# Dilated attention and S5 in one kernel: key loads as one tile for two heads, a gate unit in halves, S5's end behind each tile's weights

## The chip, the cores and the metric

The kernel runs on one core of one Trainium2 chip. The metric is the device time of one execution in microseconds (us); of the kernel before there are three runs, 2085.07, 2089.13 and 2091.08, median 2089.13 us.

The engines are named as in the profile: PE (TensorE, matrix products), DVE (VectorE), ACT (ScalarE), POOL (GpSimd) and SP (SyncE, which here only issues DMA transfers).

## The reference

Two transformer blocks stand one behind the other, both with width 1024 and 1024 positions. The first has dilated attention beside a Hyena branch, the second an S5 branch beside latent attention (MLA). What the change touches, cut down:

```python
# first block: 8 heads of 64, three dilations (window, step): (128, 1), (512, 4), (2048, 16)
for g, (window, d) in enumerate(DILATED_GROUPS):
    o_g, lse_g = dilated_window_attention(q[:, :, g], k[:, :, g], v[:, :, g], slopes, d, window // (2 * d))
wts = softmax(stack(lses))                      # weighs the three dilations against each other
y_attn = einsum(wts, stack(outs)) * silu(g_attn)
merged = sigmoid(r_attn) * (y_attn @ w_proj_attn) + sigmoid(r_hy) * (y_hy @ w_proj_hyena)
# second block
y = gelu(scan(u) + d_skip * u)                  # S5
ys = y * sigmoid(y @ w_glu + b_glu) * silu(gs)
ym = softmax(q @ k.T, causal) @ v * silu(gm)    # MLA, 4 heads, keys and values from a latent of 128
x = layer_norm(u + ple, ln_g, ln_b)
```

All is float32. The kernel forms each dense product as three products of halves (high by high, low by high, high by low); line 192 is the matmul of all of them.

## The kernel before, in words

The kernel is written in a tile language whose scheduler sorts the instructions of each engine by dependences and priorities; an engine then runs its own list in that order, and a DMA that SP can't issue yet holds all DMAs behind it. `tc.issue_after(ins)` ties what is traced under it behind an instruction on the same engine.

Dilated attention (`attention`, from about 750 to 1200 us) runs over four pairs of heads (hp 0 to 3) and in each over three dilations g. Queries, keys and values of g = 0 and 1 were projected earlier and lie in DRAM (`k.qkv`); those of g = 2 are projected in place, by products on PE that stand between the score tiles. The pool `qp` has two buffers of each tile, so the loads of (hp, 1) take the buffers of (hp-1, 2), and can start when that dilation's last scores are done. SP then issues for each head the queries (L1098, tile `qa`) and the keys' high and low halves (L1096, `kh` and `kl`), each as loads of 64 partitions by 1024 numbers, 256 KB: 4 of queries and 8 of keys.

In one dilation eight tiles of 128 queries are taken in pairs (`tp`) and for both heads: scores against `kh` and `kl` (L1170, L1171), bias and row minimum on DVE (L1172), exponential on ACT (L1175), transposes (L1182), the product with the values (L1186). Row minima and sums go to DRAM as `stat_d`: L1204 and L1208 for g = 0 and 1, L1212 for g = 2, the latter in pieces of 16 bytes. In the next head pair's first dilation the steps of `combined` read them back (L1023, tile `sn`) and weigh the dilations. After the first dilation of each head pair (`FILL`) one gate unit is traced (`r_unit`, 48 products, its tanh in two DMAs to `rs`, L984).

In the second block, `mla` (from about 1683 to 1860 us) walks through a list of steps: prepare a head (rotary queries `cs` and `qr`, L1933; `qn`, `kn`, L1911; values, L1972) or attend one block of 256 queries (row maxima L2000, exponential L2007, weights L2011, transposes by products L2024, output L2036). Behind each attended block some steps of S5's end (`s5_finish`, `others`) are traced: `fy` and `fu` (L1686, L1688, L1691) build the gelu, then four products with `w_glu` and their gates (L1699, L1703).

Of the kernel before, what the change touches and what calls it, by code (L numbers as in the profile page):

```python
# [9 lines left out]
F32 = mybir.dt.float32  # L10
F32R = mybir.dt.float32r
AF = mybir.ActivationFunctionType
ALU = mybir.AluOpType
# [3 lines left out]
P = 128  # L17
S = 1024
D = 1024
KD = D // P  # L20
# [15 lines left out]
def f(ap):  # L36
    return ap.bitcast(F32)
# [939 lines left out]
def r_unit(k, n, pool):  # L977

    u = UN["r_attn"] + n

    def evac(h, ps):
        t = pool.tile([P, 512], F32, name="tr", tag="tr")
        k.nc.scalar.activation(t, ps, AF.Tanh, scale=0.5, bias=k.hb[:, u : u + 1])
        k.nc.sync.dma_start(k.rs[n, :, h * 512 : (h + 1) * 512], t)  # L984

    unit(k, u, evac)


def attention(k):

    nc, tc, A = k.nc, k.tc, k.A
    k.yaT = [k.dram.tile([4, P, 512], F32, name="yaT%d" % b) for b in range(2)]
    with ExitStack() as es:
# [24 lines left out]
        def combined(hp, stat_d, w_d, og):  # L1018
# [47 lines left out]
                nc.sync.dma_start(k.yaT[b][hp], gt[:, b * 512 : (b + 1) * 512])  # L1066
            yield

        gts, pending = {}, iter(())
        for hp in range(4):  # L1070
            stat_d = k.dram.tile([3, S, 2, 2], F32, name="stat_d%d" % hp)
# [2 lines left out]
            for g in range(3):  # L1074
# [3 lines left out]

                r64 = [slice(0, 64), slice(64, 128)]
                qa, kh, kl = ([qp.tile([P, S], F32R, name=n + str(h)) for h in range(2)] for n in ("qa", "kh", "kl"))
                vT = qp.tile([P, S], F32, name="vT", bufs=1)

                def project(which):
                    u = (which * 3 + g) * 4 + hp
                    if u in k.qkv:
                        src = k.qkv[u]
                        if which == 2:
                            nc.sync.dma_start(vT, src[0])  # L1090
                            return
                        for h in range(2):
                            for part in range(2):
                                if which:
                                    for e in range(2):
                                        nc.sync.dma_start(f((kh, kl)[part][h][r64[e]]), src[part][r64[h]])  # L1096
                                else:
                                    nc.sync.dma_start(f(qa[h][r64[h ^ part]]), src[part][r64[h]])  # L1098
                        return
                    bias = k.b_in[:, u : u + 1]  # L1100

                    def evac(h, ps):
                        sl = slice(h * half, (h + 1) * half)
                        view = lambda t: t.rearrange("p (r l) -> p r l", r=d)[:, :, sl]
                        if which == 2:
                            evac_qkv(k, u, [view(vT)], ps, d)
                            return
                        ps = ps.rearrange("p (l r) -> p r l", r=d)
                        for x, r in enumerate(r64):
                            hi = view((qa, kh)[which][x])[r]  # L1110
                            lo = view(kl[x])[r] if which else view(qa[x])[r64[1 - x]]
                            nc.scalar.activation(hi, ps[r], AF.Identity, bias=bias[r])
                            nc.vector.scalar_tensor_tensor(lo, ps[r], bias[r], f(hi), op0=ALU.add, op1=ALU.subtract)

                    unit(k, u, evac)
                    if which == 1:
                        for t in (kh, kl):
                            for x in range(2):
                                nc.gpsimd.tensor_copy(t[x][r64[1 - x]], t[x][r64[x]])
# [34 lines left out]
                stat = st_.tile([P, 8, 2, 2], F32, name="stat", tag="stat")  # L1154
                o = op.tile([P, S], F32, name="og%d" % g, tag="og%d" % g, bufs=1 if g else 2)
                og.append(o)
                for tp in range(0, 8, 2):

                    po = ps_o.tile([P, 2, 2, P], F32, name="po", tag="po")
                    for h in range(2):  # L1160
                        ps = ps_s.tile([P, 2, 256], F32, name="s%d" % h, tag="s%d" % h)
                        sb = sp.tile([P, 2, 256], F32, name="sb", tag="sb")
                        for m in range(2):
                            t = tp + m
                            a, n, off, z, cs = tiles[t]
                            qt, ks = slice(t * P, (t + 1) * P), slice(a, a + n)
                            for e, rest in ((0, z), (z + n, len(cs) * P - z - n)):
                                if rest:
                                    nc.gpsimd.memset(sb[:, m, e : e + rest], 0.0)  # L1169
                            nc.tensor.matmul(ps[:, m, :n], qa[h][:, qt], kh[h][:, ks], start=True, stop=False)  # L1170
                            nc.tensor.matmul(ps[:, m, :n], qa[h][:, qt], kl[h][:, ks], start=False, stop=True)  # L1171
                            dve = nc.vector.tensor_tensor_reduce(sb[:, m, z : z + n], ps[:, m, :n], tabs[h][:, off : off + n],  # L1172
                                                           -0.125, 3.0e38, op0=ALU.add, op1=ALU.min,
                                                           accum_out=stat[:, t, h, 0:1])
                            act = nc.scalar.activation(sb[:, m, z : z + n], sb[:, m, z : z + n], AF.Exp, scale=-1.0,  # L1175
                                                 bias=stat[:, t, h, 0:1], accum_out=stat[:, t, h, 1:2])
                        nk = len(cs)
                        pst = ps_t.tile([P, 4, P], F32, name="pt", tag="pt")
                        pT = pt_.tile([P, 4, P], F32, name="pT", tag="pT")
                        for m in range(2):  # L1180
                            for x in range(nk):
                                nc.tensor.transpose(pst[:, m * nk + x, :], sb[:, m, x * P : (x + 1) * P], k.idn)  # L1182
                        copy(pT[:, : 2 * nk], pst[:, : 2 * nk])
                        for m in range(2):
                            for x, c in enumerate(tiles[tp + m][4]):
                                nc.tensor.matmul(po[:, h, m, :], vn[:, c, :], pT[:, m * nk + x, :],  # L1186
                                                 start=(x == 0), stop=(x == nk - 1))
                    for h in range(2):
                        hs = slice(h * 64, h * 64 + 64)
                        v, to = po[hs, h].rearrange("p m q -> p (m q)"), o[hs, tp * P : (tp + 2) * P]  # L1190
                        if g:
                            rr = d // 4
                            v = v.rearrange("p (r l) -> p r l", r=rr)
                            to = o[hs].rearrange("p (l r) -> p r l", r=d)[:, tp // 2 * rr : (tp // 2 + 1) * rr]
                        if h:
                            nc.scalar.copy(to, v)
                        else:
                            nc.vector.tensor_copy(to, v)  # L1198
                    if g == 0 and tp in (2, 4, 6):
                        with tc.issue_after(dve.ins), tc.issue_after(act.ins):  # L1200
                            next(pending, None)
# [7 lines left out]
                else:  # L1209
                    v = dst.rearrange("(l t r) c -> r l t c", r=2, t=8)  # L1210
                    for r in range(2):
                        nc.sync.dma_start(v[r], sv[r * 64 : r * 64 + 64])  # L1212

                if (hp, g) in FILL and late:
                    r_unit(k, late.pop(0), trp)
            pending = combined(hp, stat_d, w_d, og)
            if hp == 3:
                next(pending)
# [145 lines left out]
def product_half(k, w, r, h, evac):  # L1364

    wh, wl = w
    ps = k.pj.tile([P, 512], F32, name="pj", tag="pj")
    mm3(k.nc, ps, [(wh[:, q, :], wl[:, q, :], *r(q, h)) for q in range(wh.shape[1])])
    evac(h, ps)
# [498 lines left out]
def mla(k, others):  # L1868
# [3 lines left out]
    with ExitStack() as es:  # L1872
# [103 lines left out]
        def attend(h, b, shared=True):  # L1976
# [7 lines left out]
            for i in (2 * b, 2 * b + 1):  # L1984
# [23 lines left out]
                if two:  # L2008
                    nc.vector.tensor_add(mx[:, 2:3], mx[:, 2:3], mx[:, 3:4])
                nc.vector.reciprocal(mx[:, 4:5], mx[:, 2:3])  # L2010
                nc.vector.tensor_scalar(pb[:, :nk], pb[:, :nk], mx[:, 4:5], None, op0=ALU.mult)  # L2011
                pbs.append(pb)
            po = ps_o.tile([P, 256], F32, name="po", tag="po")
            for c in range(0, nkt, 2):
# [22 lines left out]
                                         stop=(last and m == 1 and x == 2))  # L2037
            nc.vector.tensor_mul(gm, gm, po)
            nc.sync.dma_start(k.mixm[b // 2][h, :, (b % 2) * 256 : (b % 2 + 1) * 256], gm)

        preparing = [prepare(h) for h in range(4)]
        for step in STEPS.split():
            h = int(step[1])
            if step[0] == "P":
                for _ in range(int(step[2])):
                    next(preparing[h], None)
            else:
                attend(h, int(step[2]))
                for _ in range(int(step[3])):
                    next(others, None)  # L2050

        for b in LASTB:
            attend(2, b, shared=False)
# [172 lines left out]
```

## Time and profile before

| | us |
|---|---|
| median of three runs | 2089.13 (2085.07 to 2091.08) |
| the profiled execution | 2090.47 |
| its span, first to last instruction | 2088.7 |
| PE busy in the span | 1972.1 (94%) |
| DVE, ACT, POOL busy | 1365.3 (65%), 833.1 (40%), 402.9 (19%) |
| mean granted TensorE clock | 0.98 of full speed |

A page of a profile gives busy times and groups of instructions; the waits view gives for each engine what it stood still for; the timeline lists instructions in order of time, with the idle time before each in brackets and the instruction or transfer that ended it. A queue row such as SPq is the issue of a DMA and not its flight.

### The profile page before, as it was taken

How to read it: one execution, taken by the hardware profiler on the slowest of the kernel's cores; microseconds unless marked ns; L12 is line 12 of the kernel's file. 1: busy time of each engine (PE TensorE's matmuls, PEld its weight loads, DVE VectorE, ACT ScalarE, POOL GpSimd, SP SyncE). 2: the span in 40 equal slices, each digit the busy share in tenths (PEclk: the TensorE clock that was granted, in tenths of full speed). 3: DMA queues.
4: the chain of work that ended last, by engine and by line, in shares of the span. 5: the costliest groups of instructions: out<-in, count | busy, mean ns of one | idle time of the engine just before them, and what ended most of it. 6: DMA issues, size and time to landing. Idle time of an engine off the chain costs nothing. (4 is left out here: it accounts for less than half of the span.)

```text
span 2088.7 us, 29820 instructions
## 1 busy us (share of the span) xinstructions
PE 1972.1 (94%) x10413; PEld 1653.3 (79%) x10413; DVE 1365.3 (65%) x2915; ACT 833.1 (40%) x1677; POOL 402.9 (19%) x434
## 2 busy tenths in 40 slices
PE   5999989999999999999899989998999989999997
PEld 3788777888888878878787877777777768788887
DVE  8797756788796224444444367766877378875776
ACT  5624333333322225545454423343323355554423
POOL 0002110232121001020202011321644242301221
PEclk9999999999999999999999999999899999999999
DMA  8245666767756473636463376353653353446351
GB/s 312 66 151 190 198 229 194 264 213 226 226 185 227 147 205 86 148 92 157 105 151 96 88 254 203 125 168 111 173 164 100 93 167 124 127 121 182 124 169 54
DMA packets 209832, 334.87 MB, mean 160 GB/s; under 512 B 51499, under 2 KB 115665, under 8 KB 209683
## 3 DMA queue, kind: packets, MB, share of 16 engines
q1 hardware_dynamic: 199744, 326.36, 51.1%
q0 software_dynamic: 1952, 4.07, 0.9%
q10 hardware_dynamic: 7986, 2.56, 0.5%
q8 instruction: 82, 1.34, 0.3%
q14 instruction: 68, 0.55, 0.1%
HBM read 251.68 MB, written 80.04 MB: 159 GB/s over the span
## 5 line engine op out<-in xcount | busy, mean ns | idle before, releaser
L192 PE MATMUL pj<-hh,wh 128*128 128x512 f32 x1104 | 436.9, 396 | 1.9 <-DVE tr L970 0.8
L192 PE MATMUL pj<-hl,wh 128*128 128x512 f32 x1104 | 436.0, 395 | 0.0
L192 PE MATMUL pj<-hh,wl 128*128 128x512 f32 x1104 | 434.7, 394 | 0.1
L177 ACT CAST wh<-raw 128x1024 fp32r<-128x1024 f32 (+3 forms) x196 | 174.9, 897 | 364.9 <-PE pj L192 299.5
L182 DVE TENSOR_TENSOR wl<-raw,wh 128x1024 fp32r<-128x1024 f32 (+2 forms) x180 | 207.4, 1154 | 122.3 <-ACT wh L177 121.8
L192 PEld LDWEIGHTS pj<-hh,wh 128*128 128x128 f32 x1104 | 209.0, 189 | 44.5 <-PE pj L192 2.6
L192 PEld LDWEIGHTS pj<-hh,wl 128*128 128x128 f32 x1104 | 208.9, 189 | 40.5 <-DVE wl L182 0.5
L192 PEld LDWEIGHTS pj<-hl,wh 128*128 128x128 f32 x1104 | 209.2, 190 | 39.5
L1172 DVE CUSTOM_DVE_ANT_0 sb<-s,tb 128x192 f32<-128x192 f32 (+2 forms) x192 | 62.4, 344 | 105.1 <-PE s L1171 84.5
L1175 ACT ACTIVATE sb<-sb,stat 128x192 f32<-128x192 f32 (+2 forms) x192 | 85.6, 447 | 82.6 <-DVE stat L1172 70.4
L192 PE MATMUL pj<-xh,wl 128*128 128x512 f32 x256 | 103.2, 403 | 1.3 <-DVE wl L182 1.3
L192 PE MATMUL pj<-xl,wh 128*128 128x512 f32 x256 | 102.0, 399 | 0.2 <-DVE xl L182 0.2
L192 PE MATMUL pj<-xh,wh 128*128 128x512 f32 x256 | 102.0, 401 | 0.0
L1186 PE MATMUL po<-pT,vn 128*128 128x128 f32 x640 | 84.2, 276 | 1.3 <-ACT pT L1016 0.8
L1186 PEld LDWEIGHTS po<-pT,vn 128*128 128x128 f32 x640 | 79.8, 191 | 5.8 <-ACT pT L1016 1.7
L1169 POOL MEMSET sb<- 128x64 f32 x80 | 9.7, 150 | 371.6 <-PE pt L1182 346.1
L821 POOL TENSOR_TENSOR zz<-zz,t 128x256 f32<-128x256 f32 x32 | 35.4, 1105 | 179.8 <-DVE t L817 140.3
L1198 DVE COPY og<-po 64x256 f32<-64x256 f32 x48 | 25.9, 539 | 66.5 <-PE po L1186 66.5
L509 DVE TENSOR_TENSOR bt<-bt 128x256 f32<-128x256 f32 x176 | 63.6, 421 | 0.4
L1170 PE MATMUL s<-kh,qa 128*128 128x192 f32 (+2 forms) x192 | 57.3, 309 | 6.2 <-DVE stat L1172 3.6
L1171 PE MATMUL s<-kl,qa 128*128 128x192 f32 (+2 forms) x192 | 53.1, 285 | 9.3 <-DMA kl<-qkv 9.3
L1182 PE MATMUL pt<-idn,sb 128*128 128x128 f32 x320 | 58.9, 282 | 0.9 <-DVE vn L1014 0.3
(605 smaller groups left out, 4570.3 us busy)
## 6 DMA issues: line engine op xcount, KB each, us to landing
raw<-in_w_in_dram SPq DMA_DIRECT2D x92, 512.0 KB, 4.1
k_fw<-k_fw SPq DMA_DIRECT2D x56, 384.0 KB, 4.5
qkv<-tr SPq DMA_DIRECT2D x80, 256.0 KB, 3.1
raw<-in_w_out_dram SPq DMA_DIRECT2D x32, 512.0 KB, 3.7
k_iv<-k_iv SPq DMA_DIRECT2D x28, 384.0 KB, 4.2
row<-in_w_ada_dram SPq DMA_DIRECT2D x16, 512.0 KB, 8.8
dc<-in_k_decay_dram SPq DMA_DIRECT2D x64, 128.0 KB, 3.6
spec<-sp SPq DMA_DIRECT2D x32, 256.0 KB, 5.2
```

The lines of the kernel that those rows point to most:

```text
L177: nc.scalar.copy(hi, src)
L182: (nc.vector if lo_eng == "dve" else nc.gpsimd).tensor_sub(lo, src, f(hi))
L192: nc.tensor.matmul(ps, a, b, start=(i == 0), stop=(i == n - 1))
L509: self.nc.vector.tensor_tensor(out, a, b, op=op)
L821: nc.gpsimd.tensor_sub(zz[:, 0], zz[:, 0], t2[:, 1])
L1170: nc.tensor.matmul(ps[:, m, :n], qa[h][:, qt], kh[h][:, ks], start=True, stop=False)
L1171: nc.tensor.matmul(ps[:, m, :n], qa[h][:, qt], kl[h][:, ks], start=False, stop=True)
L1172: dve = nc.vector.tensor_tensor_reduce(sb[:, m, z : z + n], ps[:, m, :n], tabs[h][:, off : off + n], -0.125, 3.0e38, op0=ALU.add, op1=ALU.min,
L1175: act = nc.scalar.activation(sb[:, m, z : z + n], sb[:, m, z : z + n], AF.Exp, scale=-1.0, bias=stat[:, t, h, 0:1], accum_out=stat[:, t, h ...
L1182: nc.tensor.transpose(pst[:, m * nk + x, :], sb[:, m, x * P : (x + 1) * P], k.idn)
L1186: nc.tensor.matmul(po[:, h, m, :], vn[:, c, :], pT[:, m * nk + x, :], start=(x == 0), stop=(x == nk - 1))
L1198: nc.vector.tensor_copy(to, v)
```

## The change

It has three parts. First, the gate unit of `FILL` becomes a generator of two halves (`r_halves`), whose steps are traced ahead of the tile pairs tp = 2 and 4 of the first dilation, and no longer behind it.

Second, `load_operands` allots `kh` and `kl` as one tile each for both heads and fills them with 4 loads of 64 partitions by 2 by 1024 numbers (512 KB) where 8 of 256 KB stood. The loads of (hp, 1) are traced inside the first dilation, ahead of that dilation's `stat_d` transfers and of the step that reads `sn`. SP has 32 DMAs fewer (1141 instructions, 1173 before).

Third, `attend` hands back its last instruction on the weights (`weighted`), and the steps of S5's end are traced under `tc.issue_after` of it.

```diff
+def r_halves(k, n, pool):
+    u = UN["r_attn"] + n
+    w = weights(k, "w_in", u, KD, lo_eng=k.wlo)
...
+    for h in range(2):
+        product_half(k, w, lambda q, h: (k.hh[h][:, q], k.hl[h][:, q]), h, evac)
+        yield
...
+        def load_operands(hp, g):
+            qa = [qp.tile([P, S], F32R, name="qa%d" % h) for h in range(2)]
+            ks2 = [qp.tile([P, 2, S], F32R, name=n) for n in ("kh", "kl")]
...
+                        nc.sync.dma_start(f(qa[h][r64[h ^ part]]), q[part][r64[h]])
...
+                        nc.sync.dma_start(f(ks2[part][r64[e]]), kk[part].rearrange("(h r) s -> r h s", h=2))
...
-                qa, kh, kl = ([qp.tile([P, S], F32R, name=n + str(h)) for h in range(2)] for n in ("qa", "kh", "kl"))
+                if (hp, g) not in operands:
+                    operands[hp, g] = load_operands(hp, g)
+                qa, ks2 = operands.pop((hp, g))
+                kh, kl = ([t[:, h] for h in range(2)] for t in ks2)
...
+                filler = r_halves(k, late.pop(0), trp) if (hp, g) in FILL and late else iter(())
                 for tp in range(0, 8, 2):
+                    if tp:
+                        next(filler, None)
+                    if (g, tp) == (0, 2):
+                        operands[hp, 1] = load_operands(hp, 1)
...
-                if (hp, g) in FILL and late:
-                    r_unit(k, late.pop(0), trp)
+                for _ in filler:
+                    pass
...
-                nc.vector.tensor_scalar(pb[:, :nk], pb[:, :nk], mx[:, 4:5], None, op0=ALU.mult)
+                weighted = nc.vector.tensor_scalar(pb[:, :nk], pb[:, :nk], mx[:, 4:5], None, op0=ALU.mult)
...
-                attend(h, int(step[2]))
-                for _ in range(int(step[3])):
-                    next(others, None)
+                weighted = attend(h, int(step[2]))
+                with tc.issue_after(weighted.ins):
+                    for _ in range(int(step[3])):
+                        next(others, None)
```

On SP, the place where the second head pair (hp = 1) is in its first dilation and the loads of its second dilation are issued (`qkv_6551` are its queries, `qkv_6620` its keys, `stat_d_7604` the statistics of the first head pair). Before:

```order
L1096 DMA kh_8899<-qkv_6620 64x1024 x2
L1098 DMA qa_8897<-qkv_6551 64x1024 x2
L1212 DMA stat_d_7604<-stat 512x1x4 x2
L1098 DMA qa_8898<-qkv_6551 64x1024 x2
L311 DMA raw<-in_w_in_dram 128x1024
L1023 DMA sn<-stat_d_7604 128x3x32
L1096 DMA kl_8901<-qkv_6620 64x1024 x2
L1096 DMA kh_8900<-qkv_6620 64x1024 x2
L1096 DMA kl_8902<-qkv_6620 64x1024 x2
L1090 DMA vT<-qkv_6689 128x1024
```

And now:

```order
L1094 DMA qa_8672<-qkv_6551 64x1024 x2
L1094 DMA qa_8673<-qkv_6551 64x1024
L1243 DMA stat_d_7604<-stat 512x1x4 x2
L1094 DMA qa_8673<-qkv_6551 64x1024
L1098 DMA kh<-qkv_6620 64x2x1024
L311 DMA raw<-in_w_in_dram 128x1024
L1098 DMA kh<-qkv_6620 64x2x1024
L1098 DMA kl<-qkv_6620 64x2x1024 x2
L1038 DMA sn<-stat_d_7604 128x3x32
L1124 DMA vT<-qkv_6689 128x1024
```

The queries stand ahead of the keys, all keys of both heads stand ahead of `sn`, and one key load of both heads stands on either side of a weight load. Before, the first pair of key loads stood ahead of `sn` and the other three pairs behind it. The third and fourth head pair have the same sequence, the third with one key load and `raw` in other places.

On PE at the same place, the first scores of the second dilation (`s_8937` and `s_8960` are the two heads' score tiles before). Before:

```order
L1170 MATMUL s_8937<-kh_8899,qa_8897 128x192
L1171 MATMUL s_8937<-kl_8901,qa_8897 128x192
L1186 MATMUL po<-pT,vn 128x128 x4
L1170 MATMUL s_8960<-kh_8900,qa_8898 128x192
L1171 MATMUL s_8960<-kl_8902,qa_8898 128x192
L1182 MATMUL pt<-idn,sb 128x128 x4
L1170 MATMUL s_8937<-kh_8899,qa_8897 128x192
L1171 MATMUL s_8937<-kl_8901,qa_8897 128x192
L1182 MATMUL pt<-idn,sb 128x128 x2
L1170 MATMUL s_8960<-kh_8900,qa_8898 128x192
L1171 MATMUL s_8960<-kl_8902,qa_8898 128x192
```

And now (`s_8911` and `s_8934` are the two heads' tiles):

```order
L1201 MATMUL s_8911<-kh,qa_8672 128x192
L1202 MATMUL s_8911<-kl,qa_8672 128x192
L1217 MATMUL po<-pT,vn 128x128 x4
L1213 MATMUL pt<-idn,sb 128x128 x2
L1201 MATMUL s_8934<-kh,qa_8673 128x192
L1202 MATMUL s_8934<-kl,qa_8673 128x192
L1213 MATMUL pt<-idn,sb 128x128 x2
L1201 MATMUL s_8911<-kh,qa_8672 128x192
L1202 MATMUL s_8911<-kl,qa_8672 128x192
L1201 MATMUL s_8934<-kh,qa_8673 128x192
L1202 MATMUL s_8934<-kl,qa_8673 128x192
L1213 MATMUL pt<-idn,sb 128x128 x2
```

One pair of transposes moved ahead of the second head's first scores, the rest is in the same order; the projection products (L192) follow behind the last row shown in both. The gate unit's products stand in both kernels at the same places, from the second head pair on, between the tiles of the third dilation of the head pair before.

On DVE, where the first latent head is prepared (`cs`, `qr`, `qn`), S5's steps `hbg` and `fy` stood among its instructions. Before:

```order
L1675 TENSOR_SCALAR hbg<-cols 128x4
L182 TENSOR_TENSOR wl<-raw,wh 128x512
L1933 SCALAR_TENSOR_TENSOR cs_15945<-sc,cs_15945 128x512
L1860 SCALAR_TENSOR_TENSOR t<-t,g 128x1024
L1933 SCALAR_TENSOR_TENSOR cs_15965<-sc,cs_15965 128x512
L1933 SCALAR_TENSOR_TENSOR cs_15955<-sc,cs_15955 128x512
L1686 SCALAR_TENSOR_TENSOR fy<-fu,cols,fy 128x512
L1933 SCALAR_TENSOR_TENSOR cs_15980<-sc,cs_15980 128x512
L182 TENSOR_TENSOR qr_15924<-cs_15945,qr_15924 64x512
L1686 SCALAR_TENSOR_TENSOR fy<-fu,cols,fy 128x512
L182 TENSOR_TENSOR qr_15925<-cs_15945,qr_15925 64x512
L1911 SCALAR_TENSOR_TENSOR qn_15989<-sc,qn_15988 128x512
```

And now they start behind the weights (L2041) of the first attended block:

```order
L2041 TENSOR_SCALAR pb_16055<-pb_16055,mx 128x896
L2039 TENSOR_TENSOR mx<-mx 128x1
L2040 RECIPROCAL mx<-mx 128x1
L2041 TENSOR_SCALAR pb_16078<-pb_16078,mx 128x1024
L1705 TENSOR_SCALAR hbg<-cols 128x4
L1716 SCALAR_TENSOR_TENSOR fy<-fu,cols,fy 128x512 x2
```

S5's further steps (`fu`, the products with `w_glu`) follow later by as much, and meet the old order again in the middle of the latent attention.

## Rows read from the trace of the kernel before

**Rows 1.** The page, busy time, share of the span and instructions by engine.

```profile
PE 1972.1 (94%) x10413; PEld 1653.3 (79%) x10413; DVE 1365.3 (65%) x2915; ACT 833.1 (40%) x1677; POOL 402.9 (19%) x434
```

**Rows 2.** Windows: start:end, length, each engine's busy time, clock, DMA share, GB/s.

```profile
850.00:900.00 50.00, 44.60 (x270) 38.36 (x269) 22.92 (x91) 26.88 (x81) 1.49 (x12) 0.93 0.54 116
1700.00:1750.00 50.00, 45.81 (x255) 39.77 (x255) 41.70 (x92) 27.11 (x71) 19.24 (x17) 0.93 0.27 83
1750.00:1800.00 50.00, 47.08 (x280) 40.17 (x279) 45.98 (x92) 28.44 (x71) 23.03 (x21) 1.00 0.40 125
```

**Rows 3.** Waits of PE in attention: line, releaser, total us, times, longest us.

```profile
PE s L1171 <- DMA kl<-qkv: 9.3, 7, 2.4
PE s L1170 <- DVE stat L1172: 3.6, 4, 1.1
```

**Rows 4.** Timeline of SP at the second head pair: start, us, line, transfer, count.

```profile
868.40 1.09 SPq L1096 DMA_DIRECT2D kh<-qkv  x2
869.59 1.18 SPq L1098 DMA_DIRECT2D qa<-qkv  x2
871.49 1.23 SPq L1212 DMA_DIRECT2D stat_d<-stat  x2
...
878.22 0.38 SPq L1023 DMA_DIRECT2D sn<-stat_d  x1
878.70 1.09 SPq L1096 DMA_DIRECT2D kl<-qkv  x2
```

**Rows 5.** Windows at the three transitions, columns as in Rows 2.

```profile
876.00:880.00 4.00, 3.91 (x34) 3.71 (x33) 2.71 (x11) 3.29 (x12) 0.15 (x1) 1.00 0.63 56
882.00:889.00 7.00, 5.42 (x43) 4.74 (x41) 4.75 (x19) 4.58 (x14) 0.47 (x4) 1.00 1.03 217
889.00:892.00 3.00, 0.64 (x5) 0.67 (x5) 0.00 (x0) 1.70 (x4) 0.00 (x0) 0.95 1.01 258
981.00:985.00 4.00, 3.90 (x30) 3.35 (x30) 3.52 (x15) 3.92 (x12) 0.00 (x0) 1.00 0.70 82
1088.00:1092.00 4.00, 3.89 (x32) 3.69 (x33) 2.71 (x11) 3.64 (x13) 0.15 (x1) 1.00 0.86 81
```

**Rows 6.** Timeline of PE at the second head pair, idle time before in brackets.

```profile
886.59 0.27 PE L1170 MATMUL s<-kh,qa 128*128 128x192 f32 x1
...
888.66 0.33 PE L1170 MATMUL s<-kh,qa 128*128 128x192 f32 x1
891.36 0.33 PE L1171 MATMUL s<-kl,qa 128*128 128x192 f32 x1 [2.37 <-DMA kl<-qkv]
...
895.23 0.79 PE L192 MATMUL pj<-hh,wh 128*128 128x512 f32 x1
```

**Rows 7.** Timeline of SP at the third head pair.

```profile
974.43 0.45 SPq L1096 DMA_DIRECT2D kh<-qkv  x1
974.98 1.19 SPq L1098 DMA_DIRECT2D qa<-qkv  x2
```

**Rows 8.** Waits of PE in the latent attention, columns as in Rows 3.

```profile
PE po L2036 <- DVE pT L2027: 4.3, 5, 2.0
PE sc L192 <- DVE qn L1911: 3.2, 1, 3.2
...
PE sc L192 <- DVE cs L1933: 1.6, 1, 1.6
```

**Rows 9.** Timeline of DVE at the first latent head.

```profile
1692.93 0.75 DVE L1686 SCALAR_TENSOR_TENSOR fy<-fu,cols,fy 128x512 f32<-128x512 f32 x1 [2.01 <-DMA fu<-xsd]
1693.60 0.68 DVE L1933 SCALAR_TENSOR_TENSOR cs<-sc,cs 128x512 f32<-128x512 f32 x1
...
1695.51 1.50 DVE L1686 SCALAR_TENSOR_TENSOR fy<-fu,cols,fy 128x512 f32<-128x512 f32 x1 [0.17 <-DMA fu<-xsd]
...
1697.76 0.69 DVE L1911 SCALAR_TENSOR_TENSOR qn<-sc,qn 128x512 fp32r<-128x512 f32 x1
```

**Rows 10.** Timeline of ACT at the first latent head.

```profile
1697.39 0.41 ACT L177 CAST wh<-raw 128x256 fp32r<-128x256 f32 x1 [3.25 <-DMA raw<-in_w_uq_dram]
```

More of the change, by code (lines that the diff above doesn't have):

```diff
@@ L986, in r_unit, with evac @@
     unit(k, u, evac)
+def r_halves(k, n, pool):
+    u = UN["r_attn"] + n
+    w = weights(k, "w_in", u, KD, lo_eng=k.wlo)
+    def evac(h, ps):
+        t = pool.tile([P, 512], F32, name="tr", tag="tr")
+        k.nc.scalar.activation(t, ps, AF.Tanh, scale=0.5, bias=k.hb[:, u : u + 1])
+        k.nc.sync.dma_start(k.rs[n, :, h * 512 : (h + 1) * 512], t)
+    for h in range(2):
+        product_half(k, w, lambda q, h: (k.hh[h][:, q], k.hl[h][:, q]), h, evac)
+        yield
 def attention(k):
@@ L1067, in combined @@
             yield
+        r64 = [slice(0, 64), slice(64, 128)]
+        def load_operands(hp, g):
+            qa = [qp.tile([P, S], F32R, name="qa%d" % h) for h in range(2)]
+            ks2 = [qp.tile([P, 2, S], F32R, name=n) for n in ("kh", "kl")]
+            q, kk = (k.qkv.get((which * 3 + g) * 4 + hp) for which in range(2))
+            if q is not None:
+                for h in range(2):
+                    for part in range(2):
+                        nc.sync.dma_start(f(qa[h][r64[h ^ part]]), q[part][r64[h]])
+            if kk is not None:
+                for part in range(2):
+                    for e in range(2):
+                        nc.sync.dma_start(f(ks2[part][r64[e]]), kk[part].rearrange("(h r) s -> r h s", h=2))
+            return qa, ks2
+        operands = {}
         gts, pending = {}, iter(())
@@ L1077, in attention @@
                 half = 512 // d
-                r64 = [slice(0, 64), slice(64, 128)]
-                qa, kh, kl = ([qp.tile([P, S], F32R, name=n + str(h)) for h in range(2)] for n in ("qa", "kh", "kl"))
+                if (hp, g) not in operands:
+                    operands[hp, g] = load_operands(hp, g)
+                qa, ks2 = operands.pop((hp, g))
+                kh, kl = ([t[:, h] for h in range(2)] for t in ks2)
                 vT = qp.tile([P, S], F32, name="vT", bufs=1)
@@ L1087, in project @@
                     if u in k.qkv:
-                        src = k.qkv[u]
                         if which == 2:
[L1090 to L1098, printed above, removed]
+                            nc.sync.dma_start(vT, k.qkv[u][0])
                         return
@@ L2039, in attend @@
             nc.sync.dma_start(k.mixm[b // 2][h, :, (b % 2) * 256 : (b % 2 + 1) * 256], gm)
+            return weighted
         preparing = [prepare(h) for h in range(4)]
```

## The prediction

> **What bounds the kernel now.** I read the page's busy times first: PE works for 1972.1 of 2088.7 us, 94% [rows 1]. So a change that leaves PE's instructions as they are, as this one does, can give back only PE's idle time, and the half speed that idle time brings. The windows of 50 us show where that lies: 850 to 900 us has 44.60 us of PE and a granted clock of 0.93, and in the latent attention, 1700 to 1800 us, PE is busy for 45.81 and 47.08 of 50 us while DVE is busy for 41.70 and 45.98 [rows 2]. These are two different limits, so I read the waits of each stretch apart.
>
> In dilated attention PE waits longest for the keys' low halves: 9.3 us in 7 waits, then 3.6 us for the row minima [rows 3]. SP's timeline at the second head pair tells a story that is easily believed: SP issues the first keys at 868.40 and the statistics at 871.49, then reaches `sn` only at 878.22, since that must wait for the statistics to land, and the other keys follow from 878.70 on [rows 4]. PE waits at 891.36 for the last of them [rows 6]. By SP's queue, `sn` holds back the keys and the change takes that away.
>
> The windows of the DMA engines say something else [rows 5]. From 882 to 892 us they are busy all the time (share 1.03 and 1.01, the granularity of the view) at 217 to 258 GB/s. Only 876 to 880 us has slack: share 0.63 at 56 GB/s, at a time when the statistics with their 16-byte pieces and a query load are in flight. So the keys arrive when they do because the DMA engines have as much to move as they can; an earlier issue only lengthens their queue. The third and fourth head pair look alike: 0.70 and 0.86 in the slow stretch behind the statistics.
>
> In the latent attention the waits name DVE: 4.3 us for transposed weights in 5 waits, 3.2 us for `qn`, 1.6 us for `cs` [rows 8]. DVE's timeline shows S5's `fy` in the middle of the first head's chain: it waits 2.01 us for its own load and then 0.75 and 1.50 us go into two of them, with `cs` and `qn` behind [rows 9]. But ACT too stood still there, 3.25 us for a weight load, until 1697.39, with evictions queued behind it [rows 10].
>
> **The change part by part.** *The halves of the gate unit.* No product moves: on PE they stand where they stood, in the third dilation of the head pair before. The tanh and its two DMAs are the same. For this part the change does nothing, and I cost it at 0; what the first head pair's start and the start of the second block lose or gain by the reshuffled order, I can only bound: 2 us either way each, about the size of one of the waits in rows 3. I take 0 for both.
>
> *The key loads.* Three terms, for each of three transitions (second, third and fourth head pair).
>
> First, what the DMA engines' slack can give: 0.37 of 4 us, 0.30 of 4 us and 0.14 of 4 us [rows 5], 1.5 + 1.2 + 0.6 = 3.3 us at most. The statistics are issued at the same point as before, after the last exponential of the third dilation, and the slow stretch is theirs, so part of the slack stays. I take half, -1.6 us, with 0 and -3.3 as ends.
>
> Second, a later start. The one tile for both heads is free only when the second head's last scores are done, and the queries now go first. They went at 869.59 where the first keys went at 868.40, 1.19 us later, and at the third head pair at 974.98 where a key load went at 974.43 [rows 4, 7]. At the second and fourth pair one load of 256 KB less goes ahead of the statistics, and so one more behind them: 262,144 bytes at 217 to 258 GB/s are 1.0 to 1.2 us. I take 1.1 us at these two, 0 at the third: +2.2 us; ends 0 and +2.9 (1.19 twice and 0.55).
>
> Third, what PE has to do once the last key has come. Before, the first head's first scores had run at 886.59, nearly 5 us ahead of the last key, and 3.87 us after it PE was back in the projection products (891.36 to 895.23) [rows 6]. Now both heads' keys come with the same loads, so the first head's scores (0.27 us) and the product with the values behind them stand behind the last key as well: about +0.6 us each, +1.8 us for three; ends 0, if PE fills a wait with them that it has anyhow, and +3.
>
> Sum for attention: -1.6 + 2.2 + 1.8 = +2.4 us, ends -3.3 and +5.9.
>
> The Trainium skill speaks for more. Its page "DMA: Bandwidth & Descriptors", section "Bandwidth", has each transfer cost some 2.0 us and its bytes at 436 GB/s, and so wants large ones: 8 loads of 256 KB would be 8 x 2.6 = 20.8 us and 4 of 512 KB 4 x 3.2 = 12.8 us, an estimate of 8 us less at each transition. The rows don't show such a price per load when many are in flight: 217 to 258 GB/s, that is 1.0 to 1.2 us for each 256 KB with nothing on top, and the number of bytes is unchanged. So the sum goes without it.
>
> *S5's end behind the weights.* The wait for `cs` (1.6 us) should go, since `fy` with its 2.01 us of waiting and 0.75 us of work no longer stands ahead: -1.5 us. Of the 3.2 us for `qn`, DVE would give back all, but ACT's wait for the weight load until 1697.39 stays and is late next: the second eviction of `qn` now stands behind that cast. I take -1.0 us. Of the 4.3 us for transposed weights I take -1.0 us. Against that, S5's work returns later: four `fy` alone are 2 x 2.25 = 4.5 us of DVE in a stretch where it has 8.3 + 4.0 us of idle time per 100 [rows 2], and the products with `w_glu`, which could fill PE's gaps, come later too: +1.0 us. Sum -2.5 us; ends -8 (all of 3.2 + 1.6 and most of 4.3, less 1) and +5 (the 4.5 us fall on the path, nothing is given back).
>
> All together 2.4 - 2.5 = -0.1 us: 2090.4 us by the profiled execution, whose time is 2090.47. That is 1.3 us above the median of the three runs, so in their terms 2089 us, no change. The likeliest case's own range is 2082 to 2096.
>
> **The rivals.** *The keys do come earlier* (chance 0.20). If SP's wait for `sn` is what counts, three waits of 3.5 to 4 us fall away: -10.7, +1.8 for the first head's scores, and the half-speed stretches go. The window 850 to 900 us has a clock of 0.93, so 7 us at half speed; with half of that filled with work, 1.75 us is lost, and two of three such losses saved are -3.5. With -2.5 from S5 the time is 2089 - 14.9 = 2074 us. For it: the order on SP, and PE's wait for exactly these loads. Against it: DMA engines with share 1.03 behind the slow stretch.
>
> *PE stands still in one piece* (0.12, the slower side). Where the first head's scores at 886.59 no longer run ahead, PE is idle from there until the last key. If that lands later by 1.1 us and the clock is at half speed for another 3.5 us of work (1.75 us lost), each transition costs 1.1 + 0.6 + 1.75, some 3.5 us, and the late start of the loads (1.19) on top: 4.6 x 3 = 13.9 us, with S5's -2.5 us 2100 us. It decides from the point where the last key lands after about 892.5 us in the old count of time, since then nothing of the slack is regained. For it: the tile shared by the heads. Against it: the third pair lost nothing at its start.
>
> *S5's move gives all it can* (0.13): -8 + 2.4, 2083 us. *S5 comes late* (0.08): DVE, at 92% of 1750 to 1800 us, takes the returned work on its path, +5 + 2.4, 2096 us.
>
> **How the numbers follow.** No change 0.47, the keys earlier 0.20, PE in one piece 0.12, S5's two cases 0.13 and 0.08. A measurement of this kernel can tell about 0.3%, 6.3 us. Faster by more than that: 0.20, of S5's gain about half, and 0.03 of the first case, 0.30. Slower: 0.12, half of S5's late case and 0.03, 0.19. Within: 0.51. The range goes from 2076 us, which leaves out half of the first rival, to 2099 us, which leaves out most of the slower one.
>
> **What would show it.** In the profile after: the last wait for `kl` at the second head pair ends within 1.5 us of where it ended, counted from the statistics' issue, though SP issues these keys 3 to 4 us earlier; DMA share near 1 from the statistics' landing to it; one long wait of PE at each transition where there were three short ones. The products behind it begin later by 0 to 2 us. In the latent attention the waits for `cs` are gone and that for `qn` is shorter, with ACT waiting for `raw`. I am wrong in attention if the last keys land 3 us earlier, and wrong in the latent attention if its stretch changes by more than 5 us.

## The result and the profile after

The changed kernel takes 2113.16 us, median of four runs (2108.77 to 2117.91); the kernel before, beside it, 2087.10 us (four runs, 2084.25 to 2091.08). The ratio is 1.0128, with a 95% interval from 1.0107 to 1.0149: slower by 26 us, where no change was forecast and the range ended at 2099 us. The profiled execution is the fastest of the four, 2108.77 us with a span of 2107.0 us. PE does the same work in a longer span (page, busy time by engine; before, [rows 1]):

```profile
PE 1968.8 (93%) x10413; PEld 1656.7 (79%) x10413; DVE 1367.6 (65%) x2915; ACT 833.0 (40%) x1677; POOL 403.7 (19%) x434
```

PE runs 10413 matmuls in both kernels, and outside a few swaps the n-th of one is the n-th of the other. So the place of the loss can be read by subtracting their start times, row against row. The changed kernel is 1.4 us ahead when attention begins (before's 737.7 us) and 21.7 us behind when it ends (1187.9 us): attention loses 23 us. At the first head of the latent attention 4.5 us come back and are lost again within 80 us; the stretch ends where it began. Near the end the distance is 18 us.

The windows that answer to [rows 2] (start:end, length, busy time by engine, granted clock, DMA share, GB/s) show the same: 850 to 900 us has 40.85 us of PE where it had 44.60, and 1000 to 1050 us, where the third head pair's transition now lies, has 39.09 us at a clock of 0.90, 10.9 us of standing still (that transition cost 5.1 us before, from 990 to 1004 us).

```profile
850.00:900.00 50.00, 40.85 (x256) 35.99 (x255) 18.71 (x77) 23.62 (x72) 1.02 (x8) 0.93 0.57 132
1000.00:1050.00 50.00, 39.09 (x231) 33.96 (x232) 25.42 (x72) 21.08 (x55) 11.17 (x20) 0.90 0.41 100
```

PE's waits in attention have changed their name. What was a wait for keys (9.3 us in 7) and for row minima (3.6 us) in [rows 3] is now (line, releaser, total, times, longest):

```profile
PE s L1201 <- DVE stat L1203: 27.8, 3, 9.9
PE s L1202 <- DMA kl<-qkv: 5.4, 2, 3.7
```

Three waits for DVE make 27.8 us, one for each transition from a head pair's first dilation to its second. The first of them on PE's timeline (start, us, idle time before in brackets), where [rows 6] had a wait of 2.37 us:

```profile
888.11 0.38 PE L1213 MATMUL pt<-idn,sb 128*128 128x128 f32 x2
896.87 0.53 PE L1201 MATMUL s<-kh,qa 128*128 128x192 f32 x1 [8.38 <-DVE stat L1203]
```

PE wants a score tile's place back, which DVE frees when it has read the row minima. DVE's timeline at that time shows why it does not:

```profile
885.89 0.69 DVE L1029 COPY pT<-pt 128x512 f32<-128x512 f32 x1
895.87 0.19 DVE L1047 TENSOR_TENSOR mm<-sn 128x16 f32<-128x16 f32 x1 [9.29 <-DMA sn<-stat_d]
...
896.40 0.41 DVE L1203 CUSTOM_DVE_ANT_0 sb<-s,tb 128x256 f32<-128x256 f32 x1
```

DVE is not busy. It stands 9.29 us at L1047, the first use of `sn` in the combining of the head pair before, and only then comes to the scores' L1203 that stands behind. All such waits of DVE in attention:

```profile
DVE mm L1047 <- DMA sn<-stat_d: 30.3, 3, 10.8
```

Before, DVE waited 4.2 us in two for the same read-back, 1.5 us at the second head pair and 2.7 us behind the fourth. SP's queue, against [rows 4], shows where `sn` now stands:

```profile
872.57 1.75 SPq L1094 DMA_DIRECT2D qa<-qkv  x3
874.68 1.23 SPq L1243 DMA_DIRECT2D stat_d<-stat  x2
...
876.67 0.60 SPq L1098 DMA_DIRECT2D kh<-qkv  x1
...
877.97 0.59 SPq L1098 DMA_DIRECT2D kh<-qkv  x1
878.65 3.22 SPq L1098 DMA_DIRECT2D kl<-qkv  x2
881.97 0.69 SPq L1038 DMA_DIRECT2D sn<-stat_d  x1
```

It is issued 7.29 us after the statistics (874.68 to 881.97); that was 6.73 us before (871.49 to 878.22). The issue is hardly later, but the landing is: ahead of `sn` now lie 2 MB of keys in the same queue. The time from issue to landing, shortest, median and longest; before it is recorded for one of the four read-backs, the third head pair's:

```profile
DMA to landing us min/median/max: 3.1/3.1/3.1
```

At the second head pair before, DVE got `sn` at 883.96, 5.7 us after its issue at 878.22 [rows 4]:

```profile
883.96 0.19 DVE L1032 TENSOR_TENSOR mm<-sn 128x16 f32<-128x16 f32 x1 [1.53 <-DMA sn<-stat_d]
```

After (three of them; the fourth has no key loads ahead of it):

```profile
DMA to landing us min/median/max: 13.9/15.0/15.7
```

So the chain is: key loads ahead of `sn` in the queue, `sn` takes 8 to 13 us longer to land, DVE stops at its first use, the scores behind it on DVE wait, and PE with them. The Trainium skill's page "DMA: Bandwidth & Descriptors", section "Queues, rings and completion order", says that each DMA engine consumes the descriptors (the single moves of its transfers) of its ring (its part of a queue) in order; the landing times agree with that.

### The profile page after: what moved, and what is told of

Same layout as the page of the kernel before. It is cut to its first block, busy times and chain, and to the rows that moved or that the text cites. A ratio compares the mean times of both kernels' runs of the same rounds, so it can differ in the third digit from the quotient of the medians.

```text
span 2107.0 us, 29742 instructions
## 1 busy us (share of the span) xinstructions
PE 1968.8 (93%) x10413; PEld 1656.7 (79%) x10413; DVE 1367.6 (65%) x2915; ACT 833.0 (40%) x1677; POOL 403.7 (19%) x434
## 5 line engine op out<-in xcount | busy, mean ns | idle before, releaser
L192 PE MATMUL pj<-hh,wh 128*128 128x512 f32 x1104 | 435.6, 395 | 6.0 <-DVE kl L1139 4.7
L192 PE MATMUL pj<-hl,wh 128*128 128x512 f32 x1104 | 435.1, 394 | 0.0
L192 PE MATMUL pj<-hh,wl 128*128 128x512 f32 x1104 | 433.4, 393 | 0.1
L192 PEld LDWEIGHTS pj<-hh,wh 128*128 128x128 f32 x1104 | 208.3, 189 | 47.8 <-issue 4.9
L192 PEld LDWEIGHTS pj<-hh,wl 128*128 128x128 f32 x1104 | 208.1, 188 | 40.2 <-DVE wl L182 0.5
L192 PEld LDWEIGHTS pj<-hl,wh 128*128 128x128 f32 x1104 | 208.5, 189 | 39.3
L1203 DVE CUSTOM_DVE_ANT_0 sb<-s,tb 128x192 f32<-128x192 f32 (+2 forms) x192 | 62.3, 344 | 97.9 <-PE s L1202 92.4
L192 PE MATMUL pj<-xh,wl 128*128 128x512 f32 x256 | 102.3, 399 | 1.3 <-DVE wl L182 1.3
L192 PE MATMUL pj<-xl,wh 128*128 128x512 f32 x256 | 102.1, 399 | 0.6 <-DVE xl L182 0.6
L192 PE MATMUL pj<-xh,wh 128*128 128x512 f32 x256 | 101.3, 398 | 0.0
L1217 PE MATMUL po<-pT,vn 128*128 128x128 f32 x640 | 88.6, 285 | 1.5 <-ACT pT L1031 0.9
L1201 PE MATMUL s<-kh,qa 128*128 128x192 f32 (+2 forms) x192 | 57.9, 313 | 28.9 <-DVE stat L1203 27.8
L1201 PEld LDWEIGHTS s<-kh,qa 128*128 128x128 f32 x192 | 38.3, 200 | 31.7 <-DVE stat L1203 28.8
```

Of the source, the lines that this page charges most:

```text
L192: nc.tensor.matmul(ps, a, b, start=(i == 0), stop=(i == n - 1))
```

## The experiments

Theory A: `sn` behind the key loads lands late and blocks DVE's list. Theory B: the tile for both heads holds the first head's scores until all keys are there. Theory C: S5's move costs the time. In the list, "attention" is what a kernel's PE loses from matmul 3450 to matmul 6000 (737.7 to 1187.9 us of before) in its profiled execution against that of before; the changed kernel has +23.1 us. e1 and e7, whose attention is that of before, show +3.1 and -1.4, so a difference under some 3 us means nothing.

**e1: S5's move alone,** on the kernel before.

```diff
-                attend(h, int(step[2]))
-                for _ in range(int(step[3])):
-                    next(others, None)
+                weighted = attend(h, int(step[2]))
+                with tc.issue_after(weighted.ins):
+                    for _ in range(int(step[3])):
+                        next(others, None)
```

> The kernel before with the third part alone (S5's steps behind each tile's weights). Theory A (the statistics' read-back `sn` lands behind the key loads, and DVE, which runs its list in order, stands still for it): attention is as before, so the time is 2087 us, less or more by what the latent attention gives, within 5 us; the deficit against the kernel before that grew in attention (+23 us by the places of PE's instructions) is absent. Theory C (S5's move costs the time): 2105 us or more.

2088.22 us, ratio 1.0023 (1.0007 to 1.0038). Theory C falls. The move is no gain either: the 5.3 us that the matmuls of the first head gain are lost again 80 us later.

**e2: the changed kernel without S5's move.**

```diff
-                with tc.issue_after(weighted.ins):
-                    for _ in range(int(step[3])):
-                        next(others, None)
+                for _ in range(int(step[3])):
+                    next(others, None)
```

> The changed kernel without its third part: S5's steps are tied to nothing, as before. Theories A and B (one tile for both heads makes the first head's scores wait for all keys): 2108 to 2116 us, the three waits of PE for DVE in attention stay at 8 to 10 us. Theory C: back to about 2090 us.

2106.70 us, 1.0118 (1.0102 to 1.0134), attention +22.3, the three waits for DVE 24.3 us (longest 8.8). The loss lies in the other two parts.

**e3: `sn` on POOL's queue.**

```diff
-            nc.sync.dma_start(sn.rearrange("p g j h c -> p g (j h c)"),
+            nc.gpsimd.dma_start(sn.rearrange("p g j h c -> p g (j h c)"),
```

> The changed kernel, with the DMA of `sn` issued by POOL on its own queue, so that it no longer stands in SP's ring behind four key loads. Theory A: `sn` lands within some 5 us of the statistics (13.9 to 15.7 us from issue in the changed kernel), DVE's wait for it falls from 30.3 us in three to under 8, PE's three waits of 8.4 to 9.9 us shrink to the wait for the last key, 3 to 5 us each, and the time is 2090 to 2100 us. Theory B: `sn` lands early, but PE's waits stay, under the name of the keys, and the time stays above 2108 us.

2103.67 us, 1.0100 (1.0080 to 1.0119), attention +15.7. Both theories' numbers missed. The landing came down only to

```profile
DMA to landing us min/median/max: 9.8/10.6/10.9
```

so the other queue takes `sn` past the keys only in part; DVE still waited 19.1 us for `sn`, and PE's waits moved in part to the keys:

```profile
PE s L1201 <- DVE stat L1203: 16.9, 3, 6.2
PE s L1202 <- DMA kl<-qkv: 7.6, 5, 3.0
```

**e4: the early loads one tile pair later,** so that `sn` stands behind one key load of both heads.

```diff
-                    if (g, tp) == (0, 2):
+                    if (g, tp) == (0, 4):
```

> The changed kernel with the early loads traced one tile pair later (ahead of the third pair, and so behind the step that issues `sn`): on SP `sn` now stands behind one key load of both heads and ahead of the other three. The tile for both heads and the 512 KB loads stay. Theory A: `sn` lands 3 to 6 us earlier than in the changed kernel, PE's three waits shrink from 27.8 us to 12 to 20, the time is 2095 to 2106 us. Theory B: no change, 2108 to 2116 us.

2099.37 us, 1.0084 (1.0063 to 1.0104), attention +12.5. `sn` lands 4.9 to 8.7 us after its issue; the wait for DVE shrinks by more than theory A has it, but the keys now hold PE for longer than they did in before. Both theories have a share:

```profile
PE s L1202 <- DMA kl<-qkv: 15.6, 5, 4.8
PE s L1201 <- DVE stat L1203: 6.9, 2, 4.2
```

**e5: the shared tile and the 512 KB loads alone,** at the place of before (on the changed kernel; S5 and the gate unit as before).

```diff
-                    if (g, tp) == (0, 2):
-                        operands[hp, 1] = load_operands(hp, 1)
```

> The kernel before with the shared tile and the 512 KB loads alone; the loads stay where they were traced (behind the first dilation), the gate unit is whole, S5 as before. On SP `sn` stands ahead of three of the four key loads, as in e4. Theory A alone (late `sn`): the time is that of before, 2080 to 2090 us. Theory B (the shared tile holds the first head's scores until all keys are in): about that of e4, 2095 to 2102 us, with PE's waits under the name of the keys, 3 to 5 us at each of the three transitions. With both at work (A+B), B's part is read here: e4's +12.5 us in attention.

2104.83 us, 1.0075 (1.0049 to 1.0101), attention +16.3: more than theory B gave. The keys hold PE 16.6 us in five waits, and DVE, waiting for `sn` behind one 512 KB load, another 8.1 us:

```profile
PE s L1197 <- DMA kl<-qkv: 16.6, 5, 4.4
PE s L1196 <- DVE stat L1198: 8.1, 2, 5.1
```

**e6: the early place alone,** with a tile for each head and 256 KB loads (on the changed kernel; S5 and the gate unit as before).

```diff
-            ks2 = [qp.tile([P, 2, S], F32R, name=n) for n in ("kh", "kl")]
+            ks2 = [[qp.tile([P, S], F32R, name=n + str(h)) for h in range(2)] for n in ("kh", "kl")]
...
-                for part in range(2):
-                    for e in range(2):
-                        nc.sync.dma_start(f(ks2[part][r64[e]]), kk[part].rearrange("(h r) s -> r h s", h=2))
+                for h in range(2):
+                    for part in range(2):
+                        for e in range(2):
+                            nc.sync.dma_start(f(ks2[part][h][r64[e]]), kk[part][r64[h]])
```

> The kernel before with the early place of the loads alone: one tile for each head, 8 key loads of 256 KB, traced ahead of the statistics' transfers and of `sn`, which on SP stands behind all of them. Theory A: DVE waits for `sn` 7 to 10 us at each transition and PE three times 5 to 9 us for DVE, the time is 2095 to 2105 us. Theory B alone: no slower than before, 2080 to 2090 us. A+B: A's part is read here, 8 to 14 us.

2095.48 us, 1.0043 (1.0024 to 1.0061), attention +9.0, as theory A has it for its part. PE's matmuls in attention stand in the order of before at every place, so this is what the early place alone costs. The keys are hardly waited for any more, and DVE takes their place:

```profile
PE s L1199 <- DVE stat L1201: 21.7, 3, 8.1
...
PE s L1200 <- DMA kl<-qkv: 1.1, 2, 0.8
```

**e7: the gate unit in halves alone,** on the kernel before.

```diff
+                filler = r_halves(k, late.pop(0), trp) if (hp, g) in FILL and late else iter(())
                 for tp in range(0, 8, 2):
+                    if tp:
+                        next(filler, None)
...
-                if (hp, g) in FILL and late:
-                    r_unit(k, late.pop(0), trp)
+                for _ in filler:
+                    pass
```

> The kernel before with the gate unit in halves alone. All theories: the instructions of every engine stand in the order of before, so the time is the same within 0.3%, 2078 to 2092 us.

2086.40 us, 1.0001 (0.9987 to 1.0015). The part does nothing.

**e8: the changed kernel with the combining later.** `sn` is fetched as before, its first use on DVE stands behind the second dilation's first tile pair.

```diff
-                    if g == 0 and tp in (2, 4, 6):
+                    if (g, tp) in ((0, 2), (1, 0), (1, 2)):
```

> The changed kernel with the combining steps on DVE traced later: `sn` is still fetched after the second tile pair and lands as late as before, but its first use on DVE is tied behind the first tile pair of the second dilation and the next step behind the second. Theory A: DVE no longer stands still ahead of the scores, PE's waits for DVE fall from 27.8 us to under 10 and what remains is the wait for the last key; 2095 to 2106 us. Theory B alone: no change, 2108 to 2116 us. If the chain behind `sn` (weights to DRAM and back, the product with the outputs) then stops the second dilation instead, the time stays above 2106 us under another name.

2085.77 us, 0.9997 (0.9981 to 1.0013), attention -1.7: better than theory A's number, the whole loss is gone. Not all of that is `sn`: e10 will show that the edit gives 7.4 us for another reason. The edit leaves the transfers alone, and `sn` lands as late as in the changed kernel; DVE now waits 2.8 us for it, once:

```profile
  DMA sn<-stat_d: 2.8, 1
...
DMA to landing us min/median/max: 13.7/14.6/15.5
```

The scores' waits for DVE have left the list, and what remains carries the keys' name:

```profile
PE s L1202 <- DMA kl<-qkv: 13.4, 4, 5.4
...
PE s L1201 <- DMA kh<-qkv: 2.6, 1, 2.6
```

**e9: e6 with the same late combining.**

```diff
-                    if g == 0 and tp in (2, 4, 6):
+                    if (g, tp) in ((0, 2), (1, 0), (1, 2)):
```

> e6 (one tile for each head, 256 KB loads, traced early, so that SP issues them ahead of `sn`) with e8's late combining steps. If late `sn` on DVE was all that e6 lost, its 9 us in attention go and the earlier issue of the keys shows bare: by the prediction's account (the DMA engines are full) the last key lands no more than 2 us earlier than in before, counted from the statistics' issue (19.7 us there), and the time is 2082 to 2088 us; if the early issue does bring the keys, they land 3 to 4 us earlier and the time is 2070 to 2078 us.

2079.43 us, 0.9972 (0.9959 to 0.9985), attention -6.3: faster than both kernels, and in neither of the two ranges of time expected. The keys' way can now be read without DVE in front. At the second head pair the last load of the low halves, the one PE waits for, went at 881.8 before, 10.3 us after the statistics [rows 4], and goes at 877.9 in e9, 8.1 us after them (issues of the low halves, before and in e9: count, shortest, median and longest in ns, start of the first and the last; then e9's statistics):

```profile
L1096 SPq DMA_DIRECT2D kl<-qkv x4: 450/565/1072, 878.7 to 881.8; - x4
L1099 SPq DMA_DIRECT2D kl<-qkv x4: 445/587/662, 873.1 to 877.9; - x4
869.80 1.23 SPq L1241 DMA_DIRECT2D stat_d<-stat  x2
```

PE gets the last key at 888.67, 18.87 us after the statistics' issue:

```profile
888.67 0.33 PE L1200 MATMUL s<-kl,qa 128*128 128x192 f32 x1 [1.88 <-DMA kl<-qkv]
```

Before that was 19.87 us (871.49 to 891.36) [rows 4, 6]. Issued 2.2 us earlier, landed 1.0 us earlier. e8, which has the changed kernel's loads, shows it more sharply: statistics at 870.81, last load of the low halves at 876.6, 4.5 us earlier than before, and PE gets the last key after 20.5 us, 0.6 us later than before.

```profile
870.81 1.23 SPq L1243 DMA_DIRECT2D stat_d<-stat  x2
L1098 SPq DMA_DIRECT2D kl<-qkv x2: 574/638/702, 874.8 to 876.6; - x2
891.31 0.50 PE L1202 MATMUL s<-kl,qa 128*128 128x192 f32 x1 [4.03 <-DMA kl<-qkv]
```

PE's waits in e9:

```profile
PE s L1200 <- DMA kl<-qkv: 6.2, 6, 2.1
PE s L1199 <- DVE stat L1201: 2.7, 2, 1.5
```

**e10: the kernel before with the late combining alone.**

```diff
-                    if g == 0 and tp in (2, 4, 6):
+                    if (g, tp) in ((0, 2), (1, 0), (1, 2)):
```

> The kernel before with the late combining steps alone; loads and tiles as before. DVE waited only 4.2 us for `sn` there, in two waits, and PE 3.6 us for row minima behind it: 0 to 4 us faster, 2080 to 2088 us.

2078.89 us, 0.9967 (0.9952 to 0.9982), attention -7.4, more than DVE's 4.2 us of waiting and 1 us under the range expected. The gain is not that waiting: by the matmuls' places it lies at the third head pair, between 970 and 1080 us of before, where DVE did not wait for `sn` at all. The edit has also re-sorted PE's list (942 of the 2550 matmuls in attention have another in their place), and the third head pair's statistics now go 97.8 us after the second's, where it was 105.4 us. Before, then e10:

```profile
976.91 1.23 SPq L1212 DMA_DIRECT2D stat_d<-stat  x2
...
867.65 1.23 SPq L1212 DMA_DIRECT2D stat_d<-stat  x2
965.45 1.23 SPq L1212 DMA_DIRECT2D stat_d<-stat  x2
```

Some 7 us of PE's work that stood ahead of these statistics now stands behind them, and PE, which waited 4.3 us for keys at that transition, does not wait there for any. e8, e9 and e11 have the same -7.4 us at this place, so they are to be compared with e10 and not with before. e9 has e10's order on PE and is as fast: the early place of the loads, without harm, is worth nothing that these runs can tell. The waits of e10:

```profile
PE s L1171 <- DMA kl<-qkv: 6.5, 6, 1.9
PE s L1170 <- DVE stat L1172: 2.2, 2, 1.3
```

**e11: e5 with the late combining.**

```diff
-                    if g == 0 and tp in (2, 4, 6):
+                    if (g, tp) in ((0, 2), (1, 0), (1, 2)):
```

> e5 (shared tile and 512 KB loads, at the place of before) with the late combining steps. Theory A+B: of e5's 16 us in attention the waits for DVE (8.1 us in two) go, the waits for keys (16.6 + 2.6 us in six) stay: 2092 to 2100 us. If the keys' waits go as well, they too came from DVE: 2084 to 2090 us.

2087.85 us, 1.0010 (0.9995 to 1.0025), attention +3.4, 10.8 us behind e10. The waits for keys stay, as A+B has it; the time lies in the other range because of the 7.4 us that e10 has too. The 10.8 us are the own cost of the shared tile and its 512 KB loads, which no run separates:

```profile
PE s L1197 <- DMA kl<-qkv: 13.3, 4, 4.6
PE s L1196 <- DMA kh<-qkv: 9.3, 2, 5.2
```

## Why the prediction was wrong

**The step that failed** is the sum for the key loads. It had three terms (the DMA engines' slack, a later start, PE's work behind the last key) and none for what the loads were moved past. The prediction saw `sn` only as what holds back the keys. It did not ask, turned round, what holds back `sn` when the keys go first, who reads it, and what stands behind that reader: DVE's combining (L1032 of the kernel before), which comes ahead of the scores' row minima on an engine that runs its list in order. That term shows as the 27.8 us of waits for DVE. Alone it costs 9.0 us in attention (e6). In the changed kernel it is about 17 us of the 23: with the late combining on both sides the change costs 5.7 us there (e8 against e10) and no longer 23.1. By head pair, the first to the fourth, the change cost 4.6, 6.2, 4.8 and 7.5 us, and with the late combining 3.0, 0.5, 0.0 and 2.1 us. The rival on the slower side, PE idle in one piece at each transition, foresaw the picture and 2100 us, but put it down to the last key; the piece ended with `sn`.

**Right:** at the second head pair the DMA engines, not SP's queue, set when the keys arrive. The prediction gave at most 1.5 us for an issue 3 to 4 us earlier; the last key comes 1.0 us earlier for 2.2 us in e9 and 0.6 us later for 4.5 us in e8. So the chosen view of the DMA engines' share [rows 5] held against the more obvious one of SP's queue. And the halves do nothing (e7).

**Mis-sized:** the tile for both heads. The terms "later start" (+2.2 us) and "PE's work behind the last key" (+1.8 us) made 4.0 us; with DVE out of the way the tile with its larger loads costs 10.8 us in attention where the loads stay in place (e11 against e10) and 4.6 us where they are early (e8 against e9). The last key comes 20.5 us after the statistics' issue in e8 and 24.3 us in e11, against 18.9 in e9 and 19.9 in both e10 and before. The bound of +5.9 us for the whole sum was too low for that. Why the last key lands 4.4 us later in e11 than in e10 is open: tile and load size changed together, and between the statistics and the last key the DMA engines moved 182 GB/s in e11 and 210 GB/s in e10. The first head pair, taken as 0 with 2 us either way, lost 4.6 us in the changed kernel, again in a wait for `kl` (3.7 us), as in e5 (4.1 us) and not in e6.

The price for each transfer that the prediction takes from the Trainium skill's page "DMA: Bandwidth & Descriptors" stands there as a fit in the section "Anatomy of one DMA — SWDGE (gpsimd) path", for DMAs that GpSimd issues; these loads are SP's. Half as many loads, twice as large and into one tile, came out slower here, not faster.

**S5:** -2.5 us was forecast. PE's wait for `cs` is gone and that for `qn` is 2.6 us in place of 3.2 [rows 8], as said, but S5's returned work makes a new wait, for DVE's `u` (L1941, the next head's keys and queries), of 4.2 us (e1 has it too, e2 not):

```profile
PE sc L192 <- DVE u L1941: 4.2, 2, 2.6
PE sc L192 <- DVE qn L1941: 2.6, 2, 1.5
```

Its net is nothing by the matmuls' places, and e1 is 0.23% slower. Why e1's median is 4.5 us up while its latent attention ends level is not settled.

In the order of the numbers: early place alone +9.0, shared tile alone +16.3, both +22.3 (e2) or +23.1; within the 3 us of noise the two add up. Counted from e10, with the late combining, they are +1.1 (e9), +10.8 (e11) and together +5.7 (e8): there the early place gives back about half of what the tile costs. Why is not shown.

## What to carry to other kernels

When a transfer is moved forward in a queue, list what it is moved past, then who reads that, and what stands behind the reader on its engine: a small read-back behind 2 MB of loads came 8 to 13 us later here, and an engine that runs in order passes the delay on to work that has nothing to do with it. Moving the reader, one line, took away about 17 of the 23 us in attention, where another queue (e3) and a later place of the loads (e4) took 7 and 11. But an edit of one line can re-sort a whole list: the 7.4 us that it also gave came with that, and only the same edit on the kernel before (e10) tells the two apart. And where the DMA engines are busy all the time, an earlier issue buys little.

## What the runs showed of the hardware

A queue of its own got `sn` past the keys only in part: issued by POOL it landed after 9.8 to 10.9 us, by SP behind them after 13.9 to 15.7 us. Without 2 MB of keys ahead of it SP's took 3.1 us (DMA share 0.69), and behind the fourth head pair DVE had it 2.1 us after the issue (share 0.16). The Trainium skill's page "DMA: Bandwidth & Descriptors" has, under "Rules for kernel authors", that queues of different issuers share the same DMA engines; these numbers agree.
